# A feed-forward whose gate and up products give features on partitions instead of tokens

## The chip, the core and the metric

The kernel runs on one core of a Trainium2 chip. The metric is the device time of one execution in microseconds; the median of three runs before the change is 2248.01 us (2247.26 to 2249.32).

## The reference, cut to what matters

Two blocks run one after the other on 256 tokens of 1024 features, all in float32. The first has two layers, each with a feed-forward, a mixing stage (three kinds of attention) and a second feed-forward; the second block has two layers of its own (mixing, memory attention, mixture of experts). The change touches the four feed-forwards of the first block:

```python
def rms_norm(x, w):
    xf = x.astype(jnp.float32)
    y = xf * lax.rsqrt(jnp.mean(xf * xf, axis=-1, keepdims=True) + NORM_EPS)
    return (y * w.astype(jnp.float32)).astype(x.dtype)
def swiglu(x, w_gate, w_up, w_down):
    return (jax.nn.silu(x @ w_gate) * (x @ w_up)) @ w_down
...
    for l in range(DEPTH):
        h = rms_norm(x, ffn1_norm[l])
        x = x + 0.5 * swiglu(h, ffn1_w_gate[l], ffn1_w_up[l], ffn1_w_down[l])
...
        h = rms_norm(x, ffn2_norm[l])
        x = x + 0.5 * swiglu(h, ffn2_w_gate[l], ffn2_w_up[l], ffn2_w_down[l])
```

D_MODEL is 1024, D_FF is 2816, and w_gate, w_up and w_down are 1024x2816, 1024x2816 and 2816x1024.

## The kernel before

**Products.** Every float32 operand of a large product is split into a high and a low part (`whi`, `wlo` for weights, two halves of `xt` for activations), and `mm3` (L339 to L342) makes three matmuls of the parts: high by high, high by low, low by high. `xt` holds x transposed, features on partitions, as eight blocks k of 128 features by 256 tokens; the norm's weight is multiplied in there, its root is not, and is applied to the results. The two halves h of the tokens (128 each) are separate. x, the residual, has tokens on partitions, in four tiles (h, j) of 128 by 512.

**Weights.** One stream of requests loads all weights in the order of use. A unit is 1024 columns on 128 partitions, 512 KB (`raw`); ScalarE copies it to `whi` (L296), VectorE subtracts to get `wlo` (L275). `tick()` stands between groups of matmuls; each call lets the spawned generators go on by one step and offers one split (`pump`), which is done while fewer than six split units are open. There are five rooms for raw units and seven for split ones. All four compute engines take their instructions in the order in which the program writes them.

**The feed-forward** (`gated`, called by `ffn`) goes over chunks of the 2816 features, `CUTS`: one of 512, one of 256, four of 512. In a chunk, `into` makes the gate product into two banks of tag "mm", one for each h, with x stationary and up to 512 columns of weights moving; ScalarE applies silu with the root as scale (L589); then `down` multiplies the chunk before by w_down into four banks of "accA" and "accB"; then the up product goes into two banks of "tp", and VectorE multiplies it by the root and the silu (L592). The result u has tokens on partitions, and w_down needs features there: `turned` (L536) transposes it in blocks of 128 by 128 on TensorE (L541), within the next gate product, and splits it (L544, L545). In the first chunk the three partial products are made one after the other (L514), since x comes late. In the last chunk, `last_down` ends the four sums one after the other, twelve matmuls apart, and starts for each a generator `renew`, which updates x (L616, factor 0.5), transposes it (L415), and writes the next `xt` (L426, L428) and the sum of squares (L445).

**Work between chunks.** `between[c]()` is called before the gate product of chunk c. In the first feed-forward it makes the constants of the mixing: at 1 loads, at 2 small transposes and a product (`distances`, L679), at 3, 4 and 5 two products of 512 columns each, copied to `nbias` by VectorE (`bias`, L697 to L702). In the last one it prepares the memory: at 2 to 5 four transposes of `stage` each (L1342), with a copy by ScalarE (L422) and a subtraction by VectorE (L423). All of these take their PSUM banks from tag "mm", which has two, given out in turn; a bank is free again when its last reader is done. Chunk 5's step also splits a small table.

**Order.** TensorE, VectorE, ScalarE and GpSimd follow the program's own order (`manual_schedule`); a reader that is late holds up all that is behind it on its engine.

Of the kernel before, what the change touches and what calls it, by code (L numbers as in the profile page):

```python
# [10 lines left out]
FT = mybir.dt.float32  # L11
# [12 lines left out]
NH = 2  # L24
# [18 lines left out]
ME = 9, 12, 20  # L43
P0 = (0,), (0,)
FN = 9, 9, 2, 4
CUTS = [512, 256, 512, 512, 512, 512]
CAP = 64
BIG = 1e30

# [20 lines left out]
def the_kernel(  # L70
# [83 lines left out]
    def tbank():  # L154
        return bank("tp").rearrange("p (k t) -> p k t", t=P)
# [183 lines left out]
    def mm3(o, xh, xl, wh, wl, first, last):  # L339
        nc.tensor.matmul(o, xh, wh, start=first, stop=False)  # L340
        nc.tensor.matmul(o, xh, wl, start=False, stop=False)  # L341
        nc.tensor.matmul(o, xl, wh, start=False, stop=last)  # L342
# [152 lines left out]
        return xt, rs  # L495


    def gated(xt, ready, chunks, scale, factor, last=True, renew=None, between={}, up="tp"):

        ys = []

        def into(tag, halves, hooks, done):
            W = Taken()
            o = [bank(tag)[:, :W.n] for _ in range(NH)]
            if halves == "start":

                for i, parts in enumerate(((0, 0), (0, 1), (1, 0))):
                    for h in range(NH):  # L510
                        finish(*ready[h])
                        for u in range(W.count):
                            for k in W.ks(u):
                                nc.tensor.matmul(o[h], xt.at(h, k)[parts[0]], W(k)[parts[1]], start=i == k == 0,  # L514
                                                 stop=i == 2 and k == KD - 1)
                            if i == 2 and h:
                                W.close(1)
                            if i == 2 and u == W.count - 1:
                                done(h, o[h])
                            tick()  # L520
                return
            order = [(h, u) for h in range(NH) for u in range(W.count)] if halves else \
                [(h, u) for u in range(W.count) for h in range(NH)]
            for i, (h, u) in enumerate(order):
                for k in W.ks(u):
                    mm3(o[h], *xt.at(h, k), *W(k), k == 0, k == KD - 1)
                if h:
                    W.close(1)
                if u == W.count - 1:
                    done(h, o[h])  # L530
                tick()
                for at, f in hooks:
                    if at == i + 1:
                        f()

        def turned(h, u, n):  # L536

            tp = tbank()
# [3 lines left out]
            uh = t2(FR).rearrange("p (f t) -> p f t", t=P)  # L542
            ul = t2(FR).rearrange("p (f t) -> p f t", t=P)
            nc.scalar.activation(uh[:, :nf], tp[:, :nf], AF.Copy)  # L544
            nc.vector.tensor_sub(ul[:, :nf], tp[:, :nf], uh[:, :nf].bitcast(FT))  # L545
            return uh, ul

        def down(c, ut):
            W = Taken()
            if not ys:  # L550
                ys.extend([bank(ACC[h]) for _ in range(2)] for h in range(NH))
            for f in range(W.kt):
                for h in range(NH):
                    for j in range(2):
                        mm3(ys[h][j], *(t[:, f] for t in ut[h]), *W(f, j), c == 0 and f == 0, False)
                    if h:
                        W.close(1)
                    tick()

        def last_down(c, ut, gs):  # L560
            W = Taken()
            if not ys:
                ys.extend([bank(ACC[h]) for _ in range(2)] for h in range(NH))
            for h in range(NH):
                for j in range(2):
                    for f in range(W.kt):
                        mm3(ys[h][j], *(t[:, f] for t in ut[h]), *W(f, j), c == 0 and f == 0, last and f == W.kt - 1)
                        if (h, j) == (1, 1):
                            W.close(1)
                        if h == j == 0 and f == 1:  # L570
                            ut[1] = turned(1, late[1], late[2])
                        if f == W.kt - 1 and renew:
                            gs[h].append(spawn(renew(h, j, ys[h][j])))
                        if f % 2:
                            tick()

        ut, u, gs, late = {}, [None, None], [[], []], [None] * 3
        for c in range(chunks):
            if c in between:
                between[c]()  # L580
            hooks = []
# [3 lines left out]
            ss = [None, None]  # L585
# [9 lines left out]
            n = ss[0].shape[-1]  # L595
            if c:
                down(c - 1, ut)
                ut = {}

            if c < chunks - 1:  # L600
# [6 lines left out]
        last_down(chunks - 1, ut, gs)  # L607
        return ys, gs

    def ffn(xt, rs, ready, start, between={}):  # L610

        nxt = start()
        r = lambda h: rs[h][:, 0:1]

        def renew(h, j, y):
            return nxt[-1](h, j, lambda xs: nc.vector.scalar_tensor_tensor(xs, y, 0.5, xs, op0=OP.mult, op1=OP.add))  # L616

        _, gs = gated(xt, ready, len(CUTS), r, r, renew=renew, between=between)
        return (*nxt[:-1], gs)


    def mixing_constants(fb, tmp):
# [1487 lines left out]
```

## Time and profile before

| | |
|---|---|
| median of three runs | 2248.01 us |
| the profiled execution | 2247.94 us, its span 2246.2 us |
| TensorE, matmul rows | 2143.4 us, 95% |
| TensorE, weight loads | 1570.5 us, 70% |
| VectorE | 1140.0 us, 51% |
| ScalarE | 911.8 us, 41% |
| GpSimd | 198.2 us, 9% |
| DMA | mean 218 GB/s |

The shares are means over stages. In the stages of the first block TensorE is nearly always busy and DMA moves some 110 to 250 GB/s; in the experts, near the end, DMA moves up to 394 GB/s. In the profile PE stands for TensorE's matmuls, PEld for its weight loads, DVE for VectorE, ACT for ScalarE, POOL for GpSimd. A matmul's record begins when it starts and overlaps the next.

### The profile page before, as it was taken

The numbers are of one execution on the slowest core, as the hardware profiler recorded it, in microseconds if no ns is written. First come the engines' busy times: TensorE is split into PE (matmuls) and PEld (weight loads), VectorE is DVE, ScalarE is ACT, GpSimd is POOL, SyncE is SP. The second block draws the span as 40 slices with busy tenths as digits, with TensorE's granted clock in tenths as the row PEclk, the third lists the DMA queues.
The fourth block names the chain that finished last, engine by engine and source line by source line (L and its number), as shares of the span: only waits on it lengthen the run. The fifth ranks groups of instructions, "written<-read, shape, count | busy, mean of one in ns | idle before, by whom it ended". The sixth has DMA issues, their size and how long they took to land. (4 is left out here: it accounts for less than half of the span.)

```text
span 2246.2 us, 29426 instructions
## 1 busy us (share of the span) xinstructions
PE 2143.4 (95%) x11081; PEld 1570.5 (70%) x11081; DVE 1140.0 (51%) x2024; ACT 911.8 (41%) x1453; POOL 198.2 (9%) x239
## 2 busy tenths in 40 slices
PE   8999989999999999899999999989998899979997
PEld 7778878788888888787888887953333677944332
DVE  5545886554555457866555558441111567431112
ACT  5435565454454445654544454421111454421111
POOL 1000200100000001002100002021000211020000
PEclk9999999999999999999999999999999999999999
DMA  7654453556556545435755546549999837459998
GB/s 250 200 173 150 155 157 116 176 179 198 180 173 189 190 148 172 146 111 176 241 193 182 174 145 206 188 135 382 393 394 381 288 114 261 134 209 380 393 394 308
DMA packets 240222, 490.52 MB, mean 218 GB/s; under 512 B 17680, under 2 KB 44992, under 8 KB 240064
## 3 DMA queue, kind: packets, MB, share of 16 engines
q1 hardware_dynamic: 240064, 488.48, 64.5%
q8 instruction: 91, 1.49, 0.3%
q14 instruction: 67, 0.55, 0.1%
HBM read 487.35 MB, written 1.07 MB: 217 GB/s over the span
## 5 line engine op out<-in xcount | busy, mean ns | idle before, releaser
L275 DVE TENSOR_TENSOR wlo<-raw,whi 128x1024 fp32r<-128x1024 f32 (+1 forms) x520 | 629.0, 1226 | 308.1 <-ACT whi L296 300.8
L296 ACT ACTIVATE whi<-raw 128x1024 fp32r<-128x1024 f32 x524 | 541.0, 1051 | 307.4 <-PE accB L342 116.7
L1925 PE MATMUL mm<-raw,xg 128*64 128x512 f32 x1024 | 251.5, 602 | 6.1 <-DMA raw<-in_w_up_dram 4.8
L340 PE MATMUL accB<-whi,xt 128*128 128x512 f32 (+3 forms) x448 | 175.9, 393 | 0.0
L1925 PEld LDWEIGHTS mm<-raw,xg 128*64 128x64 f32 x1024 | 72.0, 137 | 137.6 <-issue 108.3
L342 PE MATMUL accB<-whi,xt 128*128 128x512 f32 (+3 forms) x448 | 166.0, 370 | 0.0
L341 PE MATMUL accB<-wlo,xt 128*128 128x512 f32 (+3 forms) x448 | 165.6, 370 | 0.0
L340 PE MATMUL tp<-whi,xt 128*128 128x512 f32 (+1 forms) x384 | 143.6, 374 | 0.0
L342 PE MATMUL tp<-whi,xt 128*128 128x512 f32 (+1 forms) x384 | 143.4, 374 | 0.0
L341 PE MATMUL tp<-wlo,xt 128*128 128x512 f32 (+1 forms) x384 | 142.6, 371 | 0.0
L1950 PE MATMUL mm<-raw,t 128*64 128x512 f32 x512 | 122.6, 620 | 9.6 <-DVE t L1942 9.3
L340 PE MATMUL mm<-whi,xt 128*128 128x512 f32 (+1 forms) x320 | 121.2, 379 | 1.4 <-DVE nbias L702 0.7
L342 PE MATMUL mm<-whi,xt 128*128 128x512 f32 (+1 forms) x320 | 118.3, 370 | 0.0
L341 PE MATMUL mm<-wlo,xt 128*128 128x512 f32 (+1 forms) x320 | 117.7, 368 | 0.0
L342 PEld LDWEIGHTS accB<-whi,xt 128*128 128x128 f32 x448 | 84.4, 188 | 15.1
L340 PEld LDWEIGHTS accB<-whi,xt 128*128 128x128 f32 x448 | 84.5, 189 | 13.6 <-issue 1.0
L1930 ACT ACTIVATE t<-mm 128x512 f32<-128x512 f32 x32 | 19.1, 598 | 183.7 <-PE mm L1925 183.7
L341 PEld LDWEIGHTS accB<-wlo,xt 128*128 128x128 f32 x448 | 84.6, 189 | 11.8
L1841 DVE TENSOR_SCALAR back<-tp 128x256 fp32r<-128x256 f32 x32 | 13.6, 425 | 154.1 <-PE tp L1838 154.1
L592 DVE SCALAR_TENSOR_TENSOR t<-tp,ss,t 128x512 f32<-128x512 f32 (+1 forms) x48 | 33.8, 703 | 105.1 <-PE tp L342 105.1
L1950 PEld LDWEIGHTS mm<-raw,t 128*64 128x64 f32 x512 | 34.2, 140 | 74.8 <-issue 51.2
L341 PEld LDWEIGHTS tp<-wlo,xt 128*128 128x128 f32 x384 | 72.1, 188 | 13.5
(525 smaller groups left out, 4068.6 us busy)
## 6 DMA issues: line engine op xcount, KB each, us to landing
raw<-in_w_gate_dram SPq DMA_DIRECT2D x128, 512.0 KB
raw<-in_w_up_dram SPq DMA_DIRECT2D x128, 512.0 KB
raw<-in_w_down_dram SPq DMA_DIRECT2D x128, 512.0 KB
raw<-in_w_in_dram SPq DMA_DIRECT2D x120, 512.0 KB
raw<-in_ffn_w_gate_dram SPq DMA_DIRECT2D x88, 512.0 KB
raw<-in_ffn_w_up_dram SPq DMA_DIRECT2D x88, 512.0 KB
raw<-in_ffn_w_down_dram SPq DMA_DIRECT2D x88, 512.0 KB
raw<-in_w_out_dram SPq DMA_DIRECT2D x32, 512.0 KB
```

What stands on the lines that cost most here:

```text
L275: eng.tensor_sub(lo, r, hi.bitcast(FT))
L296: nc.scalar.activation(hi, r, AF.Copy)
L340: nc.tensor.matmul(o, xh, wh, start=first, stop=False)
L341: nc.tensor.matmul(o, xh, wl, start=False, stop=False)
L342: nc.tensor.matmul(o, xl, wh, start=False, stop=last)
L592: nc.vector.scalar_tensor_tensor(ss[h], o, factor(h), ss[h], op0=OP.mult, op1=OP.mult)
L1841: nc.vector.tensor_scalar(bk, tp, 0.0, None, op0=OP.is_gt)
L1925: nc.tensor.matmul(p[half(i)], xgs[e // 4][k // 4][:, k % 4, e % 4], W.whole(k, i), start=k == 0, stop=k == KD - 1)
L1930: nc.scalar.activation(c[e], p, AF.Copy)
L1950: nc.tensor.matmul(p[half(j)], uu[e][:, f], W.whole(f)[:, j * 512:(j + 1) * 512], start=f == 0, stop=f == 3)
```

## The change

All chunks behind the first have 256 features. In these, `into_turned` keeps 128x128 blocks of the weights stationary and moves x's 256 tokens, so gate and up come out with features on partitions: the two banks of a product belong to the two feature blocks f, no longer to the token halves, and the blocks alternate within each k. u then needs no transposes; `at` cuts token halves out of it for w_down. Only the first chunk still has tokens on partitions and is turned. With features on partitions the root varies along the free dimension, so a table `roots` (128 by 256) is made once by two float32 matmuls and a copy; VectorE multiplies gate by it (L619) before the silu (L621). The up factor's root is left out and comes in with the residual update, whose 0.5 becomes 0.5 times the root (L646). The last chunk does its up product one feature block after the other, and `last_down` ends its sums after the 4th, 5th, 6th and 8th group of three.

```diff
-CUTS = [512, 256, 512, 512, 512, 512]
+CUTS = [512] + 9 * [256]
...
-    def gated(xt, ready, chunks, scale, factor, last=True, renew=None, between={}, up="tp"):
-        def into(tag, halves, hooks, done):
+    def gated(pool, xt, ready, chunks, rs, renew, between):
+        ys = [[bank(ACC[h]) for _ in range(2)] for h in range(NH)]
+        def into(tag, done, ordered):
             o = [bank(tag)[:, :W.n] for _ in range(NH)]
-            if halves == "start":
+            if ordered:
...
-            order = [(h, u) for h in range(NH) for u in range(W.count)] if halves else \
-                [(h, u) for u in range(W.count) for h in range(NH)]
-            for i, (h, u) in enumerate(order):
...
-                for at, f in hooks:
-                    if at == i + 1:
-                        f()
-        def turned(h, u, n):
-            nf = n // P
-            for f in range(nf):
-                nc.tensor.transpose(tp[:, f], u[:, f * P:(f + 1) * P], ident)
...
+        def into_turned(tag, done, hook=None, in_turn=False):
+            W = Taken()
+            o = [bank(tag)[:, :S] for _ in range(2)]
+            for fs in ((0,), (1,)) if in_turn else ((0, 1),):
+                for u in range(W.count):
+                    for k in W.ks(u):
+                        xh, xl = xt.both(k)
+                        for f in fs:
+                            wh, wl = (t[:, f * P:(f + 1) * P] for t in W(k))
+                            mm3(o[f], wh, wl, xh, xl, k == 0, k == KD - 1)
+                            if k == KD - 1:
+                                done(f, o[f])
+                        if (k + 1) % (4 // len(fs)) == 0:
+                            tick()
+                    if 1 in fs:
+                        W.close(1)
+                    if hook and u == 0:
+                        hook()
+        def parts(u, to):
+            nc.scalar.activation(to[0], u, AF.Copy)
+            nc.vector.tensor_sub(to[1], u, to[0].bitcast(FT))
+            return to
+        def turned(h, u):
+            tp = transpose4(lambda f: u[:, f * P:(f + 1) * P])
+            return parts(tp, [t2(FR).rearrange("p (f t) -> p f t", t=P) for _ in range(2)])
+        def at(ut, h, f):
+            by_tokens, t = ut
+            if by_tokens:
+                return [v[:, f] for v in t[h]]
+            return [v[:, f * S + h * P:f * S + (h + 1) * P] for v in t]
         def down(c, ut):
             W = Taken()
-                        mm3(ys[h][j], *(t[:, f] for t in ut[h]), *W(f, j), c == 0 and f == 0, False)
+                        mm3(ys[h][j], *at(ut, h, f), *W(f, j), c == 0 and f == 0, False)
...
-        def last_down(c, ut, gs):
+        def last_down(ut):
             W = Taken()
-            for h in range(NH):
-                for j in range(2):
-                    for f in range(W.kt):
-                        mm3(ys[h][j], *(t[:, f] for t in ut[h]), *W(f, j), c == 0 and f == 0, last and f == W.kt - 1)
-                        if (h, j) == (1, 1):
-                            W.close(1)
-                        if h == j == 0 and f == 1:
-                            ut[1] = turned(1, late[1], late[2])
-                        if f == W.kt - 1 and renew:
-                            gs[h].append(spawn(renew(h, j, ys[h][j])))
-                        if f % 2:
-                            tick()
+            gs = [[], []]
+            for i, (h, j, f) in enumerate(((0, 0, 0), (0, 1, 0), (1, 0, 0), (0, 0, 1), (0, 1, 1), (1, 0, 1), (1, 1, 0),
+                                           (1, 1, 1))):
+                mm3(ys[h][j], *at(ut, h, f), *W(f, j), False, f == 1)
+                if f:
+                    gs[h].append(spawn(renew(h, j, ys[h][j])))
+                if i % 2:
+                    tick()
+            W.close()
+            return gs
+        ss, roots, silus = [None, None], [], [None]
         for c in range(chunks):
             if c in between:
                 between[c]()
-            if c:
-                n0 = u[0].shape[-1]
-                hooks = [(2, lambda: ut.update({h: turned(h, u[h], n0) for h in range(NH)}))]
-            def silu(h, o):
-                ss[h] = t2()[:, :o.shape[-1]]
-                nc.scalar.activation(ss[h], o, AF.Silu, scale=scale(h))
-            def product(h, o):
-                nc.vector.scalar_tensor_tensor(ss[h], o, factor(h), ss[h], op0=OP.mult, op1=OP.mult)
-            into("mm", "start" if c == 0 else None, hooks, silu)
...
-                into(up, None, [], product)
-            else:
-                cnt = 8 * n // UNIT
-                into(up, "up", [(cnt + max(1, cnt // 2), lambda: ut.update({0: turned(0, ss[0], n)}))], product)
-                late[1:] = [ss[1], n]
-            u = ss
+            if c == 0:
+                def silu(h, o):
+                    ss[h] = t2()
+                    nc.scalar.activation(ss[h], o, AF.Silu, scale=rs[h][:, 0:1])
+                def product(h, o):
+                    nc.vector.tensor_mul(ss[h], o, ss[h])
+                into("mm", silu, True)
+                into("tp", product, False)
+                continue
+            if c == 1:
+                p = bank("tp")[:, :S]
+                for h in range(NH):
+                    nc.tensor.matmul(p[:, h * P:(h + 1) * P], rs[h][:, 0:1].to_broadcast([P, P]), ident, start=True,
+                                     stop=True)
+                roots.append(pool.tile([P, S], FT, name="roots"))
+                nc.vector.tensor_copy(roots[0], p)
+            def silu_turned(f, o):
+                if f == 0:
+                    silus[0] = t2()
+                nc.vector.tensor_mul(silus[0][:, f * S:(f + 1) * S], o, roots[0])
+                if f:
+                    nc.scalar.activation(silus[0], silus[0], AF.Silu)
+            def product_turned(f, o):
+                v = silus[0][:, f * S:(f + 1) * S]
+                nc.vector.tensor_mul(v, o, v)
+                if f == 0:
+                    silus[1:] = [t2(FR), t2(FR)]
+                if c < chunks - 1 and f:
+                    parts(silus[0], silus[1:])
+                elif c == chunks - 1:
+                    parts(v, [t[:, f * S:(f + 1) * S] for t in silus[1:]])
+            before = {}
+            hook = (lambda: before.update({h: turned(h, ss[h]) for h in range(NH)})) if c == 1 else None
+            into_turned("mm", silu_turned, hook)
+            down(c - 1, (True, before) if c == 1 else ut)
+            into_turned("tp", product_turned, in_turn=c == chunks - 1)
+            ut = False, silus[1:]
+        return last_down(ut)
     def ffn(xt, rs, ready, start, between={}):
         nxt = start()
-        r = lambda h: rs[h][:, 0:1]
         def renew(h, j, y):
-            return nxt[-1](h, j, lambda xs: nc.vector.scalar_tensor_tensor(xs, y, 0.5, xs, op0=OP.mult, op1=OP.add))
...
+            return nxt[-1](h, j, lambda xs: nc.vector.scalar_tensor_tensor(xs, y, rs[h][:, 1:2], xs, op0=OP.mult,
+                                                                          op1=OP.add))
+        with tc.tile_pool(name="ffn", bufs=1, reuse_waits="tile") as pool:
+            return (*nxt[:-1], gated(pool, xt, ready, len(CUTS), rs, renew, between))
```

Two places where the order of instructions moves. TensorE in the last feed-forward, at the second memory step: before, the step's transposes (L1342, bank mm_10265) and the gate product of a 512 chunk, whose banks are mm_10272 and, the other again, mm_10273.

```order
L342 MATMUL tp_10190<-whi_10150,xt_7158 128x512
L1342 MATMUL mm_10265<-ident_64,stage_9826 128x128 x4
L340 MATMUL mm_10272<-whi_10168,xt_7155 128x512
L341 MATMUL mm_10272<-wlo_10169,xt_7155 128x512
L342 MATMUL mm_10272<-whi_10168,xt_7157 128x512
L340 MATMUL mm_10272<-whi_10168,xt_7155 128x512
L341 MATMUL mm_10272<-wlo_10169,xt_7155 128x512
L342 MATMUL mm_10272<-whi_10168,xt_7157 128x512
L340 MATMUL mm_10273<-whi_10168,xt_7155 128x512
```

Now (L1373 is the same transpose, mm_11393; gate has mm_11400 and mm_11401):

```order
L342 MATMUL tp_11331<-xt_8290,wlo_11240 128x256
L1373 MATMUL mm_11393<-ident_64,stage_10988 128x128 x4
L340 MATMUL mm_11400<-xt_8289,whi_11269 128x256
L341 MATMUL mm_11400<-xt_8291,whi_11269 128x256
L342 MATMUL mm_11400<-xt_8289,wlo_11270 128x256
L340 MATMUL mm_11401<-xt_8289,whi_11269 128x256
L341 MATMUL mm_11401<-xt_8291,whi_11269 128x256
L342 MATMUL mm_11401<-xt_8289,wlo_11270 128x256
```

The second bank of the gate product, the one that the step has just used, is written after three matmuls of 256 columns instead of six of 512.

VectorE at the same place: before, the products of the up factor (L592, one for each token half), weight splits (L275) and the step's subtraction (L423).

```order
L592 SCALAR_TENSOR_TENSOR t2_10137<-tp_10189,ss_9497,t2_10137 128x512
L275 TENSOR_TENSOR wlo_10243<-raw_10148,whi_10242 128x1024
L592 SCALAR_TENSOR_TENSOR t2_10146<-tp_10190,ss_9549,t2_10146 128x512
L423 SCALAR_TENSOR_TENSOR mem_9646<-mm_10265,mem_9644 128x4x128
L275 TENSOR_TENSOR wlo_10263<-raw_10166,whi_10262 128x1024
L545 TENSOR_TENSOR t2_10298<-tp_10292,t2_10297 128x512
```

Now (L625 multiplies the up factor of each feature block, L555 splits the result, L619 is the next gate by the roots):

```order
L625 TENSOR_TENSOR t2_11281<-tp_11330,t2_11281 128x256
L625 TENSOR_TENSOR t2_11281<-tp_11331,t2_11281 128x256
L555 TENSOR_TENSOR t2_11385<-t2_11281,t2_11384 128x512
L275 TENSOR_TENSOR wlo_11372<-raw_11237,whi_11371 128x1024
L423 SCALAR_TENSOR_TENSOR mem_10801<-mm_11393,mem_10799 128x4x128
L275 TENSOR_TENSOR wlo_11417<-raw_11267,whi_11416 128x1024
L619 TENSOR_TENSOR t2_11458<-mm_11400,roots_10995 128x256
L619 TENSOR_TENSOR t2_11458<-mm_11401,roots_10995 128x256
```

The split of u (L555), which stood behind the step's subtraction as L545, now stands ahead of it, and both up factors stand ahead of that.

## Rows read from the trace of the kernel before

**Rows 1.** The page: busy time of each engine, granted clock in 40 slices.
```profile
PE 2143.4 (95%) x11081; PEld 1570.5 (70%) x11081; DVE 1140.0 (51%) x2024; ACT 911.8 (41%) x1453; POOL 198.2 (9%) x239
...
PEclk9999999999999999999999999999999999999999
```

**Rows 2.** Waits of TensorE: us in all, times, longest us.
```profile
PE tp L415 <- DVE x L616: 1.9, 5, 0.4
```

**Rows 3.** Timeline of TensorE, 25 to 42 us: start us, us, engine, line, operation, tiles.
```profile
25.42 0.39 PE L340 MATMUL tp<-whi,xt 128*128 128x512 f32 x1
...
36.18 0.39 PE L342 MATMUL tp<-whi,xt 128*128 128x512 f32 x1
36.40 0.28 PE L340 MATMUL mm<-whi,xt 128*128 128x256 f32 x1
...
39.11 0.28 PE L342 MATMUL mm<-whi,xt 128*128 128x256 f32 x1
39.23 1.03 PE L541 MATMUL tp<-ident,t 128*128 128x128 f32 x8
...
40.23 0.28 PE L341 MATMUL mm<-wlo,xt 128*128 128x256 f32 x1
```

**Rows 4.** Groups by line and form, TensorE: count, busy us, mean ns.
```profile
L541 PE MATMUL tp<-ident,t 128*128 128x128 f32 x176 | 23.8, 272 | 0.0
```

**Rows 5.** Timeline of TensorE at 1441 us: eight matmuls, two records each.
```profile
1441.79 1.95 PE L1669 MATMUL mm<-eT,V 128*128 128x128 f32 x16
```

**Rows 6.** Timeline of TensorE: 48 up products of 256 columns; 24 gate products.
```profile
53.93 0.28 PE L340 MATMUL tp<-whi,xt 128*128 128x256 f32 x1
...
59.47 0.28 PE L342 MATMUL tp<-whi,xt 128*128 128x256 f32 x1
...
479.14 0.28 PE L340 MATMUL mm<-whi,xt 128*128 128x256 f32 x1
...
481.75 0.28 PE L342 MATMUL mm<-whi,xt 128*128 128x256 f32 x1
```

**Rows 7.** Timeline of TensorE: memory attention of both layers, 108 products each.
```profile
1416.32 0.28 PE L1359 MATMUL accA<-xt,whi 128*128 128x256 f32 x1
...
1428.92 0.28 PE L1361 MATMUL accA<-xt,wlo 128*128 128x256 f32 x1
...
1907.59 0.28 PE L1359 MATMUL accA<-xt,whi 128*128 128x256 f32 x1
...
1919.73 0.28 PE L1361 MATMUL accA<-xt,wlo 128*128 128x256 f32 x1
```

**Rows 8.** Timeline, 59 to 62 us, VectorE and TensorE: the distances step.
```profile
59.91 0.47 DVE L592 SCALAR_TENSOR_TENSOR t<-tp,ss,t 128x256 f32<-128x256 f32 x1
...
61.42 0.47 PE L340 MATMUL mm<-whi,xt 128*128 128x512 f32 x1 [0.55 <-DVE nsink L691]
```

**Rows 9.** Timeline, 1154 to 1160 us, all engines: a memory step.
```profile
1156.00 0.60 PE L1342 MATMUL mm<-ident,stage 128*128 128x128 f32 x4
...
1156.63 0.60 ACT L422 ACTIVATE mem<-mm 128x512 fp32r<-128x512 f32 x1 [2.13 <-PE mm L1342]
...
1157.29 0.68 DVE L423 SCALAR_TENSOR_TENSOR mem<-mm,mem 128x512 fp32r<-128x512 f32 x1
...
1158.02 0.19 PEld L340 LDWEIGHTS mm<-whi,xt 128*128 128x128 f32 x1 [0.46 <-DVE mem L423]
```

**Rows 10.** Timeline, 88 to 92 us, VectorE and TensorE: a bias step.
```profile
88.94 1.22 DVE L275 TENSOR_TENSOR wlo<-raw,whi 128x1024 fp32r<-128x1024 f32 x1
...
89.45 1.88 PE L701 MATMUL mm<-turned,turn 128*128 128x512 f32 x4
...
90.73 1.33 DVE L702 COPY nbias<-mm 128x512 f32<-128x512 f32 x2
...
91.56 0.47 PE L340 MATMUL mm<-whi,xt 128*128 128x512 f32 x1 [0.23 <-DVE nbias L702]
```

**Rows 11.** Timeline of ScalarE, 640 to 652 us: one set of copies.
```profile
647.88 1.15 ACT L426 ACTIVATE xt<-tp,col 128x128 fp32r<-128x128 f32 x4
```

More of the change, by code (lines that the diff above doesn't have):

```diff
@@ L536, in turned @@
-        def turned(h, u, n):
-            tp = tbank()
-            nf = n // P
-            for f in range(nf):
-                nc.tensor.transpose(tp[:, f], u[:, f * P:(f + 1) * P], ident)
[L542 to L546, printed above, removed]
+            for u in range(W.count):
+                for h in range(NH):
+                    for k in W.ks(u):
+                        mm3(o[h], *xt.at(h, k), *W(k), k == 0, k == KD - 1)
+                    if h:
+                        W.close(1)
+                    if u == W.count - 1:
+                        done(h, o[h])
+                    tick()
@@ new lines, in into_turned @@
+        def into_turned(tag, done, hook=None, in_turn=False):
+            W = Taken()
+            o = [bank(tag)[:, :S] for _ in range(2)]
+            for fs in ((0,), (1,)) if in_turn else ((0, 1),):
+                for u in range(W.count):
+                    for k in W.ks(u):
+                        xh, xl = xt.both(k)
[7 more added lines that the diff above has]
+                    if 1 in fs:
+                        W.close(1)
+                    if hook and u == 0:
+                        hook()
@@ L548, in down @@
         def down(c, ut):
             W = Taken()
-            if not ys:
-                ys.extend([bank(ACC[h]) for _ in range(2)] for h in range(NH))
             for f in range(W.kt):
@@ L558, in down @@
                     tick()
-        def last_down(c, ut, gs):
+        def last_down(ut):
             W = Taken()
-            if not ys:
-                ys.extend([bank(ACC[h]) for _ in range(2)] for h in range(NH))
-            for h in range(NH):
-                for j in range(2):
-                    for f in range(W.kt):
-                        mm3(ys[h][j], *(t[:, f] for t in ut[h]), *W(f, j), c == 0 and f == 0, last and f == W.kt - 1)
-                        if (h, j) == (1, 1):
-                            W.close(1)
-                        if h == j == 0 and f == 1:
-                            ut[1] = turned(1, late[1], late[2])
-                        if f == W.kt - 1 and renew:
-                            gs[h].append(spawn(renew(h, j, ys[h][j])))
-                        if f % 2:
-                            tick()
-        ut, u, gs, late = {}, [None, None], [[], []], [None] * 3
+            gs = [[], []]
[5 more added lines that the diff above has]
+                if i % 2:
+                    tick()
+            W.close()
+            return gs
+        ss, roots, silus = [None, None], [], [None]
+        ut = None
         for c in range(chunks):
@@ L594, in gated @@
-            into("mm", "start" if c == 0 else None, hooks, silu)
[L595 to L600, printed above, removed]
-                into(up, None, [], product)
-            else:
-                cnt = 8 * n // UNIT
-                into(up, "up", [(cnt + max(1, cnt // 2), lambda: ut.update({0: turned(0, ss[0], n)}))], product)
-                late[1:] = [ss[1], n]
-            u = ss
-        last_down(chunks - 1, ut, gs)
@@ L608, in gated @@
-        return ys, gs
+            if c == 0:
[9 more added lines that the diff above has]
+                p = bank("tp")[:, :S]
+                for h in range(NH):
+                    nc.tensor.matmul(p[:, h * P:(h + 1) * P], rs[h][:, 0:1].to_broadcast([P, P]), ident, start=True,
+                                     stop=True)
+                roots.append(pool.tile([P, S], FT, name="roots"))
+                nc.vector.tensor_copy(roots[0], p)
```

10 lines of the change are left out of this document (removed).

## The prediction

> **What bounds the kernel now.** I read the page first, for the engines' shares: TensorE's matmul rows cover 95% of the span, and the granted clock stands at the upper of its two levels (2.4 GHz) in every slice of the page [rows 1]. Then the table of who waited for whom on TensorE: in the feed-forwards it names only small items, the largest in any of their ends being 1.9 us in all, on the residual update at L616 [rows 2]. Last the timeline, because a record is no price: matmuls overlap, and what one costs is the distance from its start to the next one's, here called its slot. The 48 products of 512 columns that end the first chunk start at 25.42 and 36.18, so a slot is 10.76/47 = 0.229 us, though each record lasts 0.39 [rows 3]. So within a feed-forward TensorE is the chain, and every slot added or taken there counts, unless another engine makes it wait.
>
> **What the change removes on TensorE.** Each of the four feed-forwards loses 36 of its 44 transposes of u (22 feature blocks by two token halves; only the 8 of the first chunk stay), 144 in all. Their records last 272 ns [rows 4], but in the stream eight of them push the next matmul from 39.11 to 40.23; less two slots of 0.118 that is 0.88, or 0.11 each [rows 3]. 144 x 0.11 = **-15.9 us**.
>
> The Trainium skill, "TensorE: Matmul & The Clock Gate", Part 4, gives about 275 ns for one such transpose in a kernel. The record agrees, the slot does not; by 275 ns the gain would be 39.6 us.
>
> **What it adds on TensorE.** (a) Two float32 matmuls of 128 columns per feed-forward spread the root over partitions. Eight of that kind took 1.95 us [rows 5]; eight are added: **+2.0 us**.
>
> (b) The columns streamed stay equal, but gate and up are now cut into 256 columns: 4 chunks x 2 products x 48 = 384 matmuls of 512 columns become 768 of 256 in each feed-forward, 1536 become 3072 in all. A narrow slot shows two rhythms. In the feed-forwards of before it is mostly 0.118 (5.54/47 for an up product) and 0.1135 in some gate units (2.61/23) [rows 6]. The new form, weight block stationary and x moving, exists already in the memory attention: 0.1178 in one layer (12.60/107) and 0.1135 in the other (12.14/107) [rows 7]. A pair against 0.229 costs +6.7 ns at the slow rhythm, +10.3 us in all; at the fast one -1.9 ns, -2.9 us, and the 384 products that were narrow before gain another 1.7, so -4.6. I take two thirds slow, since the up products of the feed-forward sit there: a slot of 0.1164, 1536 x 3.9 ns less 0.5: **+5.5 us**.
>
> The same page, "Back-to-back issue gap", lists 262 cycles for 256 columns and 518 for 512, so a pair would lose 6 cycles, an estimated 2.5 ns and 3.8 us in all. That lies between the two rhythms of the rows; with it the sum would be 2256.4.
>
> **What it moves: the steps between chunks.** This is the largest term. Eight chunk starts of the first feed-forward and the last put other work between two chunks, and that work takes banks of tag "mm", of which there are two. The gate product then needs both. Before, its second bank came after six products of 512 columns (the first token half), 6 x 0.229 = 1.37 us later. Now it comes with the second feature block, after three of 256, 0.35 us later. And VectorE has more ahead of the copy that frees the bank: the order shown above puts both factors of the up product, the split's subtraction, which must wait for ScalarE's copy, and a weight split ahead of it, where before one factor and one weight split stood after the up product's first half.
>
> Count from the end of the up product's last slot. Second factor, 128x256: 0.47 [rows 8], starting about 0.26 behind the first, done at 0.74. ScalarE's copy of 512: as the 0.60 of L422 [rows 9], to 1.37. Subtraction of 512: nearest is L423 with 0.68, of which the last 0.08 overlap the next, to about 2.0. Weight split: 1.22 [rows 10], overlapping likewise, to 3.15. Then the step's own copy.
> - Four memory steps of the last feed-forward: four transposes (0.44), three products (0.35), so the second bank is asked for at 0.79 and free when L423's work (0.68) ends, 3.80, plus 0.05: a wait of 3.06. Before, the same work was released at 1158.02; six slots after transposes that began at 1156.00 would be 1157.81, so it already waited about 0.3 (the row's 0.46 is the weight load, issued ahead) [rows 9]. 4 x 2.7 = 10.9.
> - Three bias steps: both banks go through copies of 1.33 together; before, gate began 2.11 behind the last up product's slot (91.56 less 89.45) [rows 10]. Now the first copy ends at 3.85 and the second at 4.5, and gate runs as if begun at 4.2. 3 x 2.1 = 6.3.
> - One step of distances: before, 61.42 less 59.59 = 1.83 [rows 8]; now its small copies begin at 3.15 and gate at about 4.05: 2.2.
>
> Together **+19.4 us**. Below, the bound is one weight split less ahead of each copy (8 x 1.22 = 9.8, as if VectorE came to the split early enough); above, one more.
>
> **The ends.** The last product by w_down now ends its four sums close together. Update, transposes and next products follow in an order in which I find x ready: the waits of 1.9 [rows 2] go. But at the end of the second feed-forward the next one's first pass reaches the second token half while ScalarE has one more set of copies to do, 1.15 [rows 11]. **-0.8 us**; bounds -1.9, and 4 x 1.15 = +4.6 if each end pays that.
>
> **Edits at nothing.** Multiplying by the root table and the silu run beside the product by w_down of the chunk before (24 x 0.229 = 5.5 us); factor and split of up beside the next gate product (48 slots, 5.6 us), which is where a lost cover would cost. The update's factor from a column instead of 0.5 changes no shape. Weights have the same bytes; rows of 1 KB instead of 2 KB occur before in the 256 chunk, and its products run without a break [rows 6]. Weight splits are offered 8 times per chunk of 16.8 us and 6 are needed, each 1.22 on VectorE [rows 10]: some 10 of 16.8 us with the rest of its work, so they hold.
>
> **Sum.** -15.9 + 2.0 + 5.5 + 19.4 - 0.8 = +10.2. The profiled execution took 2247.94 us (span 2246.2); the median of the runs is 2248.01, so the two agree. 2247.94 + 10.2 = **2258.1 us**.
>
> **Rivals.** A measurement here can tell about 0.2%, 4.5 us: faster is below 2243.5, slower above 2252.5.
> - *Not slower, by the rhythm.* If all narrow slots lie at 0.1135, the slot term is -4.6 instead of +5.5 and the time 2248.0. Place: 3456 narrow products; the point is the middle of the slots, 0.1147 being where the whole change comes to +4.5. For: one layer's attention ran 107 slots so, in the same form [rows 7]. Against: the up products [rows 6]. Chance 0.14.
> - *The waits are half.* If VectorE does the weight split before the up product ends, each wait loses 1.22: 2248.3. For: it idles there. Against: the order of its instructions. Chance 0.12. Both together: 2238.2, chance 0.12.
> - *Transposes cost their record.* 144 x 0.272 = 39.2 instead of 15.9: 2234.8, faster. The rows with start times speak against it [rows 3]. Chance 0.04. (The skill's 275 ns, Part 4 as above, would say this.)
> - *Late weights.* With 8 offers per chunk one miss leaves TensorE waiting for a split of 1.22; once in each of the 36 narrow chunks is +44: 2302. Against: four units lie ready ahead. Chance 0.06.
>
> My forecast has 0.52. Slower is 0.52 + 0.06 = 0.58, same 0.14 + 0.12 = 0.26, faster 0.12 + 0.04 = 0.16. The forecast's own range is 2250 to 2269 (rhythm to +4.8, ends to +4.6). The range for 8 in 10 takes in both cases near 2248 and leaves out the late weights, the transposes' records and most of the double case: 2243 to 2269.
>
> **What would show it.** In the changed kernel's timeline: at each memory step TensorE idle for about 3 us behind three gate products, released by VectorE's L423, now at the same helper line; at each bias step some 4.2 us between last up and full gate; 864 narrow slots per feed-forward at 0.1135 to 0.118; 8 transposes left in each; feed-forwards two and three, which have no steps, shorter by 0.5 to 4.5 us each. If the first and the last feed-forward come out shorter than before, the waits were misread; if the middle two are longer, the slots were.

## The result, and the profile after

The changed kernel takes 2264.88 us (median of five runs, 2263.18 to 2272.76) against 2248.12 for the kernel before: **ratio 1.0087**, 95% interval 1.0074 to 1.0100, so slower by 17 to 22 us. The forecast was 2258.1 with a range of 2243 to 2269. The profiled execution took 2271.84 us, its span is 2270.1 against 2246.2 before: 23.9 us more.

The page of the changed kernel, answering to [rows 1]: its span, the engines' busy time, and the granted clock in 40 slices.

```profile
span 2270.1 us, 32355 instructions
...
PE 2142.1 (94%) x12489; PEld 1631.9 (72%) x12489; DVE 1169.9 (52%) x2132; ACT 899.3 (40%) x1449; POOL 196.6 (9%) x239
...
PEclk9999999999999999999989999989999999999999
```

TensorE's busy time stayed, and two slices, each 57 us long, are now below 0.9; before, none was. The table of waits on TensorE, answering to [rows 2] (us in all, times, longest us):

```profile
PE mm L340 <- DVE mem L423: 11.6, 4, 2.9
...
PE mm L340 <- DVE nbias L733: 6.2, 3, 2.1
PE tp L415 <- DVE xt L428: 5.9, 6, 1.6
...
PE mm L725 <- DVE col L170: 2.3, 1, 2.3
```

Three of these four are the steps between chunks that the forecast named. The third was not foreseen: it stands at the ends of the feed-forwards. The small item on the update [rows 2] went, as predicted.

The timeline of one memory step after, answering to [rows 9] (start us, us, engine, line, operation, tiles; in brackets the idle time before and who ended it):

```profile
1156.06 0.77 DVE L625 TENSOR_TENSOR t<-tp,t 128x256 f32<-128x256 f32 x2 [5.05 <-PE tp L342]
...
1156.21 0.60 PE L1373 MATMUL mm<-ident,stage 128*128 128x128 f32 x4
1156.56 0.37 PE L340 MATMUL mm<-xt,whi 128*128 128x256 f32 x1
...
1157.46 0.58 ACT L422 ACTIVATE mem<-mm 128x512 fp32r<-128x512 f32 x1
1157.58 0.69 DVE L555 TENSOR_TENSOR t<-t,t 128x512 fp32r<-128x512 f32 x1 [0.76 <-ACT t L554]
...
1158.19 1.22 DVE L275 TENSOR_TENSOR wlo<-raw,whi 128x1024 fp32r<-128x1024 f32 x1
1159.33 0.68 DVE L423 SCALAR_TENSOR_TENSOR mem<-mm,mem 128x512 fp32r<-128x512 f32 x1
...
1160.07 0.58 PE L340 MATMUL mm<-xt,whi 128*128 128x256 f32 x1 [2.91 <-DVE mem L423]
1160.45 0.41 PE L341 MATMUL mm<-xt,whi 128*128 128x256 f32 x1
...
1165.99 0.34 PE L340 MATMUL mm<-xt,whi 128*128 128x256 f32 x1
1166.17 0.28 PE L341 MATMUL mm<-xt,whi 128*128 128x256 f32 x1
```

Up to 1160.07 this is the forecast's list in its order: factors, ScalarE's copy, subtraction, weight split, L423, then gate's second bank, after a wait of 2.91 us (3.06 was worked out). What follows was not in it. From 1160.45 to 1165.99 the 26 slots are 5.54/26 = 0.213 us, and behind them they are short again: for these 5.5 us the granted clock was at its lower level, 1.2 GHz. At 0.1135 the same 26 slots take 2.95, so this fall cost 2.6 us, nearly as much as the wait before it. The Trainium skill, "TensorE: Matmul & The Clock Gate", Back-to-back issue gap, gives N/1.2 ns for N columns at the lower level, an estimated 213 ns for 256; the rows agree.

Where the time went, stage by stage, from the first product of a stage to that of the next (us, from the timelines of TensorE; the last four columns are experiments below):

| stage | before | after | mem_tp | steps_tp | ends | both |
|---|---|---|---|---|---|---|
| feed-forward 1 (distances, bias steps) | 202.46 | 211.24 | 209.77 | 203.24 | 208.15 | 200.99 |
| mixing | 241.36 | 245.73 | 241.72 | 244.16 | 244.13 | 242.57 |
| feed-forward 2 | 192.71 | 190.37 | 190.38 | 190.37 | 188.69 | 188.63 |
| feed-forward 3 | 189.38 | 186.11 | 187.68 | 186.11 | 184.52 | 184.18 |
| mixing | 242.99 | 241.88 | 241.94 | 241.82 | 240.31 | 241.86 |
| feed-forward 4 (memory steps) | 195.83 | 210.12 | 192.39 | 192.37 | 209.20 | 192.00 |

The two feed-forwards with steps lost 8.8 and 14.3 us, the two without gained 2.3 and 3.3. Single falls of the clock come and go between executions in stages that an edit does not touch: the 187.68 of mem_tp holds one, and the first mixing lies between 241.4 and 245.7.

### The profile page after: what moved, and what is told of

Same layout as the page of the kernel before. It is cut to its first block, busy times and chain, and to the rows that moved or that the text cites. A ratio compares the mean times of both kernels' runs of the same rounds, so it can differ in the third digit from the quotient of the medians.

```text
span 2270.1 us, 32355 instructions
## 1 busy us (share of the span) xinstructions
PE 2142.1 (94%) x12489; PEld 1631.9 (72%) x12489; DVE 1169.9 (52%) x2132; ACT 899.3 (40%) x1449; POOL 196.6 (9%) x239
## 5 line engine op out<-in xcount | busy, mean ns | idle before, releaser
L275 DVE TENSOR_TENSOR wlo<-raw,whi 128x1024 fp32r<-128x1024 f32 (+1 forms) x520 | 627.7, 1231 | 168.9 <-ACT whi L296 167.5
L340 PE MATMUL mm<-xt,whi 128*128 128x256 f32 x576 | 165.7, 288 | 18.2 <-DVE mem L423 11.6
L342 PE MATMUL mm<-xt,wlo 128*128 128x256 f32 x576 | 163.4, 284 | 0.0
L341 PE MATMUL mm<-xt,whi 128*128 128x256 f32 x576 | 163.3, 284 | 0.0
L340 PE MATMUL tp<-xt,whi 128*128 128x256 f32 x576 | 159.5, 277 | 0.0
L341 PE MATMUL tp<-xt,whi 128*128 128x256 f32 x576 | 159.3, 277 | 0.0
L342 PE MATMUL tp<-xt,wlo 128*128 128x256 f32 x576 | 159.2, 276 | 0.0
L340 PEld LDWEIGHTS mm<-xt,whi 128*128 128x128 f32 x576 | 112.7, 196 | 21.8 <-DVE mem L423 12.4
L625 DVE TENSOR_TENSOR t<-tp,t 128x256 f32<-128x256 f32 x72 | 27.9, 424 | 179.7 <-PE tp L342 179.7
L341 PEld LDWEIGHTS mm<-xt,whi 128*128 128x128 f32 x576 | 112.7, 196 | 0.0
L342 PEld LDWEIGHTS mm<-xt,wlo 128*128 128x128 f32 x576 | 112.3, 195 | 0.0
L341 PEld LDWEIGHTS tp<-xt,whi 128*128 128x128 f32 x576 | 108.3, 188 | 1.5
L340 PEld LDWEIGHTS tp<-xt,whi 128*128 128x128 f32 x576 | 108.1, 188 | 1.5
L342 PEld LDWEIGHTS tp<-xt,wlo 128*128 128x128 f32 x576 | 108.2, 188 | 0.0
L554 ACT ACTIVATE t<-t 128x512 fp32r<-128x512 f32 (+1 forms) x40 | 23.5, 589 | 184.3 <-DVE t L625 184.3
```

The source lines that it names most:

```text
L275: eng.tensor_sub(lo, r, hi.bitcast(FT))
L554: nc.scalar.activation(to[0], u, AF.Copy)
L625: nc.vector.tensor_mul(v, o, v)
```

## The experiments

All ratios are to the kernel before on the same chip, from 5 to 12 executions unless said otherwise. Differences to the changed kernel are differences of ratios, and its own interval, some 3 us either way, enters into each of them.

**Other banks for the steps (mem_tp, steps_tp).** The gate product should wait only because a step holds a bank of "mm".

```diff
-            parts = memory(memT[0], "mm", 2)
+            parts = memory(memT[0], "tp", 2)
```

steps_tp gives the products and transposes of the distances and of the bias steps "tp" banks as well.

> The changed kernel, with the four memory steps of the last feed-forward taking their banks from tag tp instead of mm; nothing else moves. Theory 1 (the gate product waits for the second mm bank, behind the two factors, the subtraction, the weight split and L423 on VectorE): the waits of 2.9 us at L340 released by L423's memory parts go; each step then keeps at most some 0.35 us for its three transposed products, so 4 x 2.6 = 10 us less, 2254 from a changed kernel of 2264. Theory 2 (the wait itself is only part; after it the granted clock falls to half for about 3.4 us, in which 44 products take 0.173 us each instead of 0.1135, 2.6 us lost at a step): 4 x (2.6 + up to 2.6) = 10 to 20 us less, 2244 to 2254, and the slices of the last feed-forward below a clock of 0.95 go. Rival (the waits would be taken over by a tp bank that the up product before still holds): a wait of the same size moves to the step's transposes, under 3 us less.

Measured: 1.0013 (1.0002 to 1.0024), 0.0074 or 16.6 us less than the changed kernel's ratio, within theory 2 and beyond what theory 1 allows. A memory step of mem_tp in its timeline:

```profile
1148.07 0.66 PE L1373 MATMUL tp<-ident,stage 128*128 128x128 f32 x4 [0.18 <-DVE t L625]
...
1148.48 0.37 PE L340 MATMUL mm<-xt,whi 128*128 128x256 f32 x1
1148.68 0.28 PE L341 MATMUL mm<-xt,whi 128*128 128x256 f32 x1
```

A wait of 0.18 on the up product's first factor is all that is left, so the rival (a wait as long on "tp") is out. The last feed-forward is 17.7 us shorter; the waits explain 11.6 less 4 x 0.18, that is 10.9. The other 6.8 is the clock. These are stretches of 10 us of the changed kernel (start:end, us, busy us of each engine with its instructions, granted clock, DMA share, GB/s):

```profile
1130.00:1140.00 10.00, 7.09 (x58) 6.89 (x57) 4.33 (x6) 3.37 (x5) 0.00 (x0) 0.94 0.24 71
1140.00:1150.00 10.00, 10.00 (x59) 9.18 (x59) 4.39 (x6) 3.48 (x4) 0.00 (x0) 0.89 0.44 135
1150.00:1160.00 10.00, 7.16 (x59) 6.79 (x58) 4.19 (x7) 4.06 (x5) 0.00 (x0) 0.96 0.68 213
1160.00:1170.00 10.00, 9.93 (x53) 9.62 (x54) 3.06 (x5) 1.16 (x2) 0.00 (x0) 0.70 0.37 109
1170.00:1180.00 10.00, 10.00 (x72) 9.24 (x71) 4.27 (x5) 3.42 (x5) 0.00 (x0) 1.00 0.63 211
1180.00:1190.00 10.00, 7.10 (x48) 6.89 (x47) 3.75 (x5) 2.97 (x4) 0.00 (x0) 0.83 0.37 105
```

and of mem_tp, where each of the six stands at 1.00; two of them:

```profile
1150.00:1160.00 10.00, 10.00 (x66) 9.02 (x66) 8.06 (x9) 5.17 (x7) 0.00 (x0) 1.00 0.78 217
1160.00:1170.00 10.00, 9.82 (x87) 9.63 (x86) 4.33 (x6) 3.84 (x5) 0.00 (x0) 1.00 0.48 155
```

The clocks missing to 1 in the six stretches of the changed kernel add to 0.68 x 10 = 6.8 us of full clock: the same number. Not every wait brings a fall: in all three profiles of the changed kernel one follows the first three waits of 2.9 us, none the fourth (it ends at 1204.78), and behind the three waits of 2.1 us at the bias steps there is only one.

> As mem_tp, and the step of distances and the three bias steps of the first feed-forward take tp banks too, so all eight steps between chunks leave the mm banks to gate. Theory 1 alone: the predicted 19.4 us go nearly whole, 17 to 19 less than the changed kernel (2245 to 2248 from 2264). Theory 2 with the clock falls: another 2 us at three or four of the steps, 22 to 30 less in all, 2234 to 2242. Rival (the two tp banks are held by up's factor and the split, so the step's products wait there as long): under 5 us less.

Measured: 0.9983 (0.9973 to 0.9992), 23.4 us less than the changed kernel, and 3.8 us faster than before. It lies at the lower end of the clock theory and above the 17 to 19 of the waits alone. Feed-forward 1 lost the 6.2 on L733 and is 8.0 us shorter; the slices at 0.90 and 0.93 between 100 and 120 us went. The distances step keeps a wait of 1.9 on its own column copy.

**The wait filled (fill).** Is it the idling that lowers the clock, or something that comes with it? The four memory steps get work that changes nothing else:

```diff
+                d = bank("tp")[:, :S]
+                for i in range(26):
+                    xh = xt.both(i % 8)[0]
+                    nc.tensor.matmul(d, xh[:, :P], xh, start=True, stop=True)
```

> The changed kernel with 26 further products of 256 columns, whose result nobody reads, in each of the four memory steps of the last feed-forward, between the transposes and gate; they go to a tp bank, and the wait for the mm bank stays as long (26 x 0.1135 = 2.95 us of it are now filled). Theory (beside the wait itself, TensorE's granted clock falls after each wait of 2.9 us, and that costs as much again): no granted clock below 0.95 from 1130 to 1200 us, the last feed-forward 7 us shorter than the changed kernel's 210.1, so 2257 against 2264, although TensorE does more. Rival (the clock's falls there have another cause, such as the DMA's rate or the load itself): the falls stay, and the time is 0 to 2 us longer than the changed kernel's.

Measured: 1.0062 (1.0049 to 1.0076), 5.6 us less than the changed kernel, with 104 products more. The two intervals overlap a little, so the stage tells more than the total. Stretches of fill at the same place:

```profile
1140.00:1150.00 10.00, 10.00 (x67) 9.11 (x67) 5.31 (x7) 3.48 (x4) 0.00 (x0) 1.00 0.54 152
1150.00:1160.00 10.00, 10.00 (x85) 9.83 (x84) 4.09 (x6) 4.05 (x5) 0.00 (x0) 1.00 0.65 213
1160.00:1170.00 10.00, 10.00 (x68) 9.16 (x67) 5.31 (x7) 3.51 (x5) 0.00 (x0) 1.00 0.51 146
```

No fall is left among the memory steps; the last feed-forward takes 204.7 us instead of 210.1 (210.0 in the two other profiles). That is 5.4 less and not 7: the 26 products took 3.2 us at a step, more than the wait that they filled. VectorE's order is as before: in fill's second memory step L423 starts 3.12 us behind the step's transposes, as it does in the changed kernel, so the wait is not shorter, only filled. Slices at 0.83 between 60 and 70 us and between 130 and 140 stand in feed-forward 1, which was not filled. So the idling brings the fall. The Trainium skill tells this of waits for DMA between bursts of products, which then start at the lower clock ("TensorE: Matmul & The Clock Gate", HAM oscillation); in this trace the wait is for a PSUM bank that VectorE holds.

**One split less ahead (no_split).** The price of the wait should follow VectorE's queue.

```diff
-                            tick()
+                            tick(split=int(tag == "mm" or k < KD - 1 or c + 1 not in between))
```

> The changed kernel without the offer of a weight split at the end of an up product that a step follows, so that VectorE comes to the step's copies (L423, L733, L170) one split of 1.22 us earlier; the same splits are done at later offers. Theory (VectorE's queue sets the wait): each memory step waits 1.7 us instead of 2.9, each bias step 1.1 less, 8 x 1.14 = 9 us less in all, and if waits of 1.7 us bring no fall of the clock, up to 8 more: 2247 to 2255 against 2264. Rival (a split is then late for a later product, since 7 offers are left for 6 splits): the gain is eaten by a wait on wlo at L340 to L342, 0 to 3 us less.

Measured: 1.0026 (1.0016 to 1.0036), 13.7 us less than the changed kernel. Waits of no_split:

```profile
PE mm L340 <- DVE mem L423: 7.1, 4, 1.8
...
PE mm L340 <- DVE nbias L733: 2.8, 3, 0.9
```

Each lost one split's time (2.9 to 1.8, 2.1 to 0.9), 7.9 us in all, with the distances' wait (2.3 to 1.2) 9.0, and among the memory steps only one fall is left, over two slices at 0.93 and 0.89. No split came late. So my "waits are half" case was the right price for another order, which this change does not have.

**The ends (ends).** The transposes of the second token half take banks that are free by then:

```diff
-                                                                          op1=OP.add))
+                                                                          op1=OP.add), ACC[j] if h else "tp")
```

with the tag passed on to `transpose4`, and `tick(split=0)` at the end of `last_down`.

> The changed kernel, with the transposes at a feed-forward's end for the second token half put into the accumulator bank that the update has just read, not into a third and fourth bank of tag tp, and one more call of the generators at the end of the last product by w_down. Theory: at each of the four ends the third transposes wait some 1.6 us for L428's split to leave a tp bank, which VectorE does behind the updates at L646; the distance from the last product by w_down to the next stage's first product, 3.9 us at three ends and 2.5 at the fourth against 0.2 at the end of the first one before, falls by 1.5 to 3 each: 6 to 12 us less in all, 2252 to 2258 from 2264, if the clock's falls behind the ends go too. Rival (VectorE's sequence of updates itself is late, not the bank): the wait stays under another name, and under 2 us are gained.

Measured: 1.0049 (1.0035 to 1.0063), 8.5 us less. The end of feed-forward 1 in the changed kernel's timeline, answering to [rows 11] for the second half:

```profile
216.60 1.40 DVE L646 SCALAR_TENSOR_TENSOR x<-accB,ss,x 128x512 f32<-128x512 f32 x2
216.65 0.40 PE L342 MATMUL accB<-whi,t 128*128 128x512 f32 x1
...
216.88 0.60 PE L415 MATMUL tp<-ident,x 128*128 128x128 f32 x4
...
217.91 2.15 DVE L428 SCALAR_TENSOR_TENSOR xt<-tp,col,xt 128x128 fp32r<-128x128 f32 x8
...
219.09 0.66 PE L415 MATMUL tp<-ident,x 128*128 128x128 f32 x4 [1.61 <-DVE xt L428]
...
220.12 0.69 PE L415 MATMUL tp<-ident,x 128*128 128x128 f32 x4 [0.38 <-DVE xt L428]
220.53 0.71 PE L340 MATMUL accA<-whi,xt 128*128 128x512 f32 x1
```

and in ends:

```profile
214.76 0.40 PE L342 MATMUL accB<-whi,t 128*128 128x512 f32 x1
...
215.51 0.66 PE L415 MATMUL accA<-ident,x 128*128 128x128 f32 x4
...
216.17 0.65 PE L415 MATMUL accB<-ident,x 128*128 128x128 f32 x4
216.58 0.48 PE L340 MATMUL accA<-whi,xt 128*128 128x512 f32 x1
```

From the last product by w_down to the next stage it is 3.88 us in the one and 1.82 in the other (0.23 in the kernel before, whose sums end farther apart). In the changed kernel the third set of transposes needs a "tp" bank, both hold the first half's x, and VectorE frees one only behind three updates.

**Both remedies (both).**

> The edits of steps_tp and ends together. If the two causes are separate, their gains add: 2264 less 17 to 30 less 6 to 12, so 2222 to 2241, faster than the kernel before (2248). If the clock's falls are what most of the excess is and one remedy removes them, less than the sum. If both are misread, it stays near 2260.

Measured: 2233.16 us, **ratio 0.9937** (0.9923 to 0.9950), 33.7 us less than the changed kernel and 14 less than before. The sum of the two alone would be 23.4 + 8.5 = 31.9, so within the noise the gains add, as separate causes would have it. This version beats both kernels.

**The same banks in the kernel before (before_tp).**

> The kernel before, with the same eight steps taking tp banks as in steps_tp. It tells how much of that remedy is owed to the change. Theory: before, a memory step waited some 0.3 us and a bias step began gate 2.1 us behind the last up product, of which its own two products need 0.5; so at most 4 x 0.3 + 3 x 1.6 + 1.4 = 7 us less, 2241 to 2247. Rival (in the kernel before, the transposes of u in gate need the tp banks, so the steps' copies hold them up instead): no gain, or some us longer, 2248 to 2254.

Measured: 0.9998 (0.9989 to 1.0007). No gain: the last feed-forward is 1.2 us shorter, but in the first one the steps now wait 1.7 us for a "tp" bank behind the up factors (L592), where gate waited 1.3 before. The remedy's 23 us pay back only what the change itself brought.

**Narrow but not turned (narrow_tokens).** The kernel before with `CUTS = [512] + 9 * [256]`.

> The kernel before with all chunks behind the first 256 wide, as after the change, but gate and up products still with tokens on partitions, x stationary and weights moving; 44 transposes of u per feed-forward stay. It tells the narrow columns from the turned form. If narrow slots with x stationary take the slow rhythm (0.118, as the up products of 256 columns in the kernel before): 1536 x 6.7 ns = 10 us more, 2258; if the fast one (0.1135): 2.9 us less and the 384 narrow products 1.7 less, 2243. The steps take their second mm bank after 12 products of 256, 1.36 us, as before; their waits grow at most by the weight split ahead, 8 x 1.2 = 10 us more on either figure.

Measured: 1.0055 (1.0042 to 1.0068), 12.4 us more than before. In the trace the gate and up products of the four feed-forwards take 8.5 us more, most of what the slow rhythm should cost. Another 5.3 come at the ends: the sums of a narrow last chunk end six products apart, and from the last product by w_down to the next stage it is 2.6 us at three ends and 0.6 at the fourth instead of 0.23. So of the 3.6 us that an end of the changed kernel lost, some 2.4 would come with the narrow chunk alone, without the turned form; the expectation had no such term. First and last of 48 up products of narrow_tokens, 5.53/47 = 0.1177, as before [rows 6]:

```profile
501.87 0.28 PE L340 MATMUL tp<-whi,xt 128*128 128x256 f32 x1
...
507.40 0.28 PE L342 MATMUL tp<-whi,xt 128*128 128x256 f32 x1
```

and of the changed kernel, 5.35/47 = 0.1138:

```profile
1150.73 0.28 PE L340 MATMUL tp<-xt,whi 128*128 128x256 f32 x1
...
1156.08 0.28 PE L342 MATMUL tp<-xt,wlo 128*128 128x256 f32 x1
```

Of the narrow slots of gate and up in the feed-forwards, those at the lower clock left out, 2653 of 3368 lie between 0.116 and 0.124 us in narrow_tokens and 263 of 3298 in the changed kernel. The fast rhythm goes with the turned form here, but the form alone does not settle it: 10 of the 36 up products of narrow_tokens run at 0.1133 throughout, and the gate product behind the distances in the changed kernel at 0.118. Why is open: the memory attention, already turned and untouched, has one layer at each rhythm before [rows 7] and both at the fast one after.

**The changed kernel twice more (again_1, again_2; one execution each).** Its five runs lie at 2263 to 2265 and at 2272, with a mean granted clock of 0.982 to 0.983 and of 0.979 to 0.980.

> The changed kernel unaltered, for a second profile: its five runs lay at two places, 2263 to 2265 and 2272, and the profiled one at 2272. Theory (falls of the granted clock, which come after the waits in some executions and not in others, make the difference): an execution near 2264 shows the same waits to 0.3 us (11.6 behind L423, 6.2 behind L733, 5.9 behind L428) and 8 us less of time in slices with a clock below 0.97, that is three to five falls fewer. Rival (a DMA or a split comes late in the slower ones): the waits differ by the 8 us.

> As again_1, a third profile: the number of ten-microsecond slices below 0.97 before 1300 us goes with the time, about 1.7 us of span for one slice at 0.83; the waits stay. Rival: the waits differ.

Measured: 2269.82 and 2268.46 us, so neither came near 2264 and the expectation could not be tried. The waits are the same to 0.1 us (11.6, 6.2, 5.9), and so are the stages up to the last feed-forward (it ends at 1295.8 and 1295.3, in the first profile at 1294.7). All three profiles have eleven falls before 1300 us; what separates 2268 from 2272 lies behind the feed-forwards. What sets the runs near 2264 apart is open; their clock, higher by 0.003 of 2264, or 7 us, fits fewer falls, but no profile shows it.

## Why the prediction was right in its sign and too low in its sum

**Right.** *The steps between chunks*: 3.06 us per memory step against 2.91; gate 4.2 behind the last up product at a bias step against 3.95 (81.79 to 85.74 below); 4.05 against 3.94 at the distances (59.52 to 63.46). With these the term is 4 x 2.55 + 3 x 1.84 + 2.1 = 17.8 instead of 19.4, and mem_tp, steps_tp and no_split show that it is the "mm" bank behind VectorE's queue. *The transposes*: no run undid them alone, but in each feed-forward the slots of the 44 take 4.23 us before and those of the 8 left 0.79: 3.4 less, 13.8 in all against 15.9. *The roots*: their two matmuls push the second gate product from 36.38, where its slot would begin, to 36.84, 0.46 per feed-forward, 1.8 against 2.0.

A bias step in the changed kernel's timeline, answering to [rows 10], and the roots' matmuls, the first rows:

```profile
36.05 0.39 PE L342 MATMUL tp<-whi,xt 128*128 128x512 f32 x1
36.27 0.61 PE L612 MATMUL tp<-ident,ss 128*128 128x128 f32 x4
36.64 0.37 PE L340 MATMUL mm<-xt,whi 128*128 128x256 f32 x1
36.84 0.28 PE L341 MATMUL mm<-xt,whi 128*128 128x256 f32 x1
...
81.79 1.88 PE L732 MATMUL mm<-turned,turn 128*128 128x512 f32 x4
...
83.78 1.22 DVE L275 TENSOR_TENSOR wlo<-raw,whi 128x1024 fp32r<-128x1024 f32 x1
84.91 1.28 DVE L733 COPY nbias<-mm 128x512 f32<-128x512 f32 x2
...
85.74 0.36 PE L340 MATMUL mm<-xt,whi 128*128 128x256 f32 x1 [2.07 <-DVE nbias L733]
```

The weight split at 83.78 stands ahead of the bias copies, as it was counted; its 1.22 is what no_split took away.

**Wrong.**
- *Slots*, the step "I take two thirds slow, since the up products of the feed-forward sit there": nearly all are fast, as in the rival "by the rhythm" with its -4.6, and not +5.5. In feed-forwards 2 and 3 gate and up take 1.3 us less each, so the term is -5.3. The row that it was nearest to was of the other form.
- *The ends*, "an order in which I find x ready": the order of x was right and the transposes' bank was left out. Transposes, roots and slots come to -4.3 in a feed-forward without steps; 2 and 3 gained 2.3 and 3.3, so an end costs +2.0 and +1.0, about +6 for four instead of -0.8.
- *The falls of the clock*, missing: I counted a wait at its own length. At the memory steps they cost 6.8; in feed-forward 1 the slices at 0.83, 0.90 and 0.93 between 60 and 120 us add to 3.4, and the one behind its end to 1.7. In all some 12 us. Such falls could be read before: the digit 9 of the page [rows 1], taken for the upper level in every slice, means 90% or more of 56 us. In the kernel before, a fall stands behind each of the two waits of 2.1 us at the end of the mixing (L415 on L1212), as the clock of these stretches shows:

```profile
450.00:460.00 10.00, 7.90 (x33) 6.08 (x32) 9.26 (x23) 6.39 (x17) 0.56 (x1) 0.83 0.52 139
...
1080.00:1090.00 10.00, 9.37 (x36) 7.63 (x37) 5.56 (x16) 1.75 (x6) 4.46 (x13) 0.83 0.94 310
```

Sum: -13.8 + 1.8 - 5.3 + 17.8 + 6 + 12 = +18.5, against the 19.6 of the ratio (16.6 to 22.5). The errors on the slots (-11) and on the other two (+19) partly cancelled, and it is by this luck that the time lies inside the range. The profiled execution has some 6 us more, in work that the change does not touch: falls between 300 and 330 us, which other kernels here show too, and 2.9 us behind the feed-forwards.

## What to carry to other kernels

Before a product is reshaped so that its second accumulator is needed earlier, list who holds that tag's banks then and what is queued ahead of the reader that frees them; a tag that is idle at that moment can take the visitors, here for 23 us. Price a wait of TensorE of 2 to 3 us, in a stretch where it is otherwise busy, at up to twice its length (here a fall followed three of four waits of 2.9 us and one of three of 2.1), and look at the granted clock behind it in short stretches. A reshaping that merely breaks even may be a gain held back by two bank choices: terms that save (transposes, slots) and terms that cost (waits) should be tested apart.

## What the runs showed of the hardware that I had not expected

Three of four waits of 2.9 us on TensorE were followed by a fall of the clock, one of them with 5.5 us of products at the lower level; 26 products of 256 columns put into each wait removed the falls and won 5.4 us in the stage. Products of 256 columns mostly have a slot of 0.118 us with weights moving and 0.1135 with x moving, in the same place of the program, with the same columns in all; some whole products of each form take the other slot, and no run shows why.
